# Where the halves of split weights are kept, and block inverses made for two token blocks at once: a hybrid decoder layer on one core

## The chip, the core and the metric

The kernel runs on one core of a Trainium2 chip. The core has five engines, each with its own in-order queue: TensorE (PE) multiplies matrices, VectorE (DVE) and ScalarE (ACT) work on elements, GpSimd (POOL) does so too, and SyncE (SP) issues the DMAs. The metric is the time of one execution on the device in microseconds (us); lower is better. The time before is a median of three runs.

## The reference

One decoder layer over 2048 tokens of width 1024. A projection of the input feeds three mixers: a gated DeltaNet of four heads (GDN), a dilated window attention and a differential attention. Their outputs go through `w_out` into a layer norm; a feed-forward stage with a short convolution and a second norm follow. The part that the change touches is the GDN, in chunks of tokens:

```python
a_mat = jnp.eye(C) + m                        # m: strictly lower, k k^T times decay
u = triangular_solve(a_mat, v * beta)         # the kernel makes the inverse of a_mat
w = triangular_solve(a_mat, k_beta * exp(g))
def step(S, inp):                             # over the chunks, in order
    v_new = u_i - w_i @ S
    o = q_i @ S + qk_i @ v_new
    S = S * exp(g_last) + k_tail.T @ v_new
```

The reference uses chunks of 64; the kernel uses chunks of 128, which computes the same.

## The kernel before

The 2048 tokens are four blocks of 512. Products are made in two parts: `Dense.weights` (L119 to L138) loads a raw weight tile of 128 x 1024 (512 KB), ScalarE casts it to a head `whi` (L132), GpSimd subtracts to get the rest `wlo` (L133), and a product (L174) sums three matmuls per 128 rows. Raw tile, head and rest come from one ring of seven buffers (`NW`). Where a weight has a key and `keep` is set, head and rest are also stored to DRAM (L137), and the next use of that key loads these two tiles (L127) and splits nothing. `keep` is set when the job A1 is reached (L1292).

The program is a list of jobs, `FIRST`, `SECOND` and `THIRD` (L1341 to L1343). An is the projection for the two attentions of block n (eight products and two rounds over four value weights), Gn the input of the GDN of block n (sixteen products with convolution, and gates), dn and wn the two attentions, o0 the product with `w_out` for block 0, c0 the opening of the feed-forward stage, t0 a transposition, fn the feed-forward stage of block n. A0 and G0 run before `keep` is set. `SECOND` also holds the jobs of the recurrence. in is the inverse: for each of the four chunks of block n it multiplies keys (L426), masks with the decay (L405 to L411), and stores the 32 x 32 diagonal blocks (L430); 64 of these (4 positions, 4 chunks, 4 heads) lie on 64 partitions (L435), and a loop of 31 steps with two DVE instructions each (L441, L443) inverts them; a transposed copy (L444) goes to the other 64 partitions, and both are stored (L446). bn merges the inverse of half a block (L488 and L489 load it, L498 to L518 multiply), pn prepares half a block (k and v transposed, q k), rn runs the two chunks of half a block one after the other: L530, L533, L537, L539, L542 and L545 make the state, L555 to L576 the output (L573 makes it, L576 stores it).

The order in the program is a priority. The framework lays down each engine's queue by it: work of a later job is put ahead where an earlier one isn't ready by its own estimate, and buffers come free as tiles are released. Small steps of a projection's end (norms, gates) are put off by some products with `Dense.put` and brought out by `Dense.flush`; the job in calls it with no number, which brings out everything. All DMAs are issued by SP in order. The PSUM banks of the recurrence (five) come free after r7, and the jobs of `THIRD` need them.

Of the kernel before, what the change touches and what calls it, by code (L numbers as in the profile page):

```python
# [7 lines left out]
F32 = mybir.dt.float32  # L8
F32R = mybir.dt.float32r
AF = mybir.ActivationFunctionType  # L10
ALU = mybir.AluOpType
# [365 lines left out]
def gdn_phase(tc, I, y_d, dn, cols, order, emit):  # L377
# [3 lines left out]
    with ExitStack() as ctx:  # L381
# [32 lines left out]
        def invert(t):  # L414

            qk_d = cols.blocks[t][0]
            ms = []
            blk_d = tc.dram_tile([4, 4 * H, 32, 32], F32, name="blk_d")
            for c in range(4):
                k = p2.tile([P, H, C], F32, tag="v", name="k", bufs=NV)  # L420
                nc.sync.dma_start(out=k, in_=qk_d[:, :, 0, c * C : (c + 1) * C])
                m = p2.tile([P, H, P], F32, tag="m0", name="m0", bufs=NM)
                decay(m, t, 0, c)
                kk = bank("kk")
                for h in range(H):
                    nc.tensor.matmul(out=kk[:, h], lhsT=k[:, h], rhs=k[:, h], start=True, stop=True)  # L426
                nc.vector.tensor_tensor(out=m, in0=kk, in1=m, op=ALU.mult)
                for b in range(4):
                    bs = slice(32 * b, 32 * b + 32)
                    nc.sync.dma_start(out=blk_d[b, c * H : (c + 1) * H].rearrange("q j i -> j q i"), in_=m[bs, :, bs])  # L430
                ms.append(m)
            xb = p2.tile([P, 32, 32], F32, tag="fx", name="fx", bufs=1)
            fs = p2.tile([P, 32, 32], F32, tag="fs", name="fs", bufs=1)
            mb, tmp = fs[0:64], fs[64:P]
            nc.sync.dma_start(out=mb, in_=blk_d.rearrange("b q j i -> (b q) j i"))  # L435
            nc.gpsimd.memset(xb[0:64], 0.0)
            nc.gpsimd.memset(xb[0:64].rearrange("p i c -> p (i c)")[:, 0:1024:33], 1.0)
            for j in range(31):
                n = 31 - j
                rows, cls = slice(j + 1, 32), slice(0, j + 1)  # L440
                nc.vector.tensor_tensor(out=tmp[:, rows, cls], in0=mb[:, j, rows].unsqueeze(2).broadcast_to([64, n, j + 1]),  # L441
                                        in1=xb[0:64, j, cls].unsqueeze(1).broadcast_to([64, n, j + 1]), op=ALU.mult)
                nc.vector.tensor_tensor(out=xb[0:64, rows, cls], in0=xb[0:64, rows, cls], in1=tmp[:, rows, cls], op=ALU.subtract)  # L443
            nc.vector.tensor_copy(xb[64:P], xb[0:64].rearrange("p i c -> p c i"))  # L444
            x_d = tc.dram_tile([2, 4, 4 * H, 32, 32], F32, name="x_d")
            nc.sync.dma_start(out=x_d, in_=xb)  # L446
            return ms, x_d
# [33 lines left out]
        def merge(turn, ms, x_d):  # L481

            xt = xts[turn % NXT]
            at = 2 * (turn % 2)
# [37 lines left out]
        def recur(t, hb, xt, qk, kn, vb, mq):  # L522
# [4 lines left out]
            for ci in range(2):  # L527
# [29 lines left out]
                junk = p2.tile([P, P], F32, tag="junk", name="junk", bufs=1)  # L557
# [21 lines left out]
        for job in order:  # L579
# [4 lines left out]
            elif job[0] == "b":  # L584
                merged[n] = merge(n, *inverse[n // 2])
            elif job[0] == "p":
                ready[n] = prepare(n // 2, n % 2)
            elif job[0] == "r":
                recur(n // 2, n % 2, merged.pop(n), *ready.pop(n))
            else:  # L590
                emit(job)
# [653 lines left out]
def decoder(tc, I, out, y_d=None, upto=3):  # L1245
    nc = tc.nc
    with ExitStack() as ctx:
# [11 lines left out]
        def emit(job):  # L1259
# [4 lines left out]
            elif job[0] == "G":  # L1264
                run(gi.project(n))
# [4 lines left out]
            elif job[0] == "c":  # L1270
                dn.flush()
                early.close()
# [13 lines left out]
        with ExitStack() as first:  # L1286
# [4 lines left out]
            for job in FIRST[1:]:  # L1291
                dn.keep = dn.keep or job == "A1"  # L1292
# [49 lines left out]
SECOND = "i0 b0 p0 b1 p1 r0 i1 p2 r1 p3 b2 r2 G2 i2 b3 b4 b5 r3 p4 G3 c0 r4 i3 p5 r5 p6 p7 b6 b7 r6 r7 A3 o0".split()  # L1342
# [79 lines left out]
```

## Time and profile before

| what | value |
|---|---|
| median of three runs | 3292.46 us (3285.46 to 3297.71) |
| profiled execution | 3287.69 us, of it span 3285.8 us |
| PE busy | 3039.0 us, 92% of the span |
| DVE, ACT, POOL busy | 1940.7, 1251.7, 493.0 us |
| bytes moved by DMA | 701.06 MB, mean 213 GB/s |

The page of the profile gives busy time per engine; matmuls overlap in it, so a matmul's own duration is longer than its share of the time. The granted clock is the share of full speed that TensorE was given. A stage is a stretch of the span; the table by stretch gives for each the busy time of the engines (in brackets the number of instructions), the granted clock, the share of time that the DMA engines were busy, and the rate. A wait names who waited and for what it waited last.

### The profile page before, as it was taken

Reading aid. Unit: us, or ns where it says so; the run is one execution under the profiler, and the core shown is the slowest. Engines: PE = TensorE matmul, PEld = TensorE weight load, DVE = VectorE, ACT = ScalarE, POOL = GpSimd, SP = SyncE. Lnnn points to the kernel's source line nnn. Section 1 sums busy time; section 2 is a strip of 40 time slices with the busy share of each in tenths; the row PEclk is TensorE's granted clock in tenths of the full one; section 3 lists DMA queues with packets and bytes.
Section 4 is the critical chain, followed back from the end, with each engine's and each line's share of the span. In section 5 each row is a group of like instructions: output and inputs, shape, how many; then the busy total and the mean of one; then the engine's idle time right before and its main releaser. Section 6 shows DMA issues by size and latency. Waiting matters only on the chain.

```text
span 3285.8 us, 41437 instructions
## 1 busy us (share of the span) xinstructions
PE 3039.0 (92%) x14476; PEld 2335.1 (71%) x14476; DVE 1940.7 (59%) x3738; ACT 1251.7 (38%) x2735; POOL 493.0 (15%) x342
## 2 busy tenths in 40 slices
PE   7888687999978888998999999999999999999998
PEld 5666576787767667666776667777788666788887
DVE  2564177858544536755887645565897444474446
ACT  2644143353324315644655422232655333221113
POOL 3452252111102003333312000000000000000001
PEclk8899898999988989999999999999999999999999
DMA  6437776766778878766785655555775444665553
GB/s 190 144 132 263 262 257 218 222 208 200 242 253 276 289 246 265 245 225 209 269 281 198 232 187 177 180 184 173 238 261 201 148 162 144 209 236 192 192 188 139
DMA packets 365281, 701.06 MB, mean 213 GB/s; under 512 B 63024, under 2 KB 189488, under 8 KB 364304
## 3 DMA queue, kind: packets, MB, share of 16 engines
q1 hardware_dynamic: 365072, 698.41, 64.0%
q8 instruction: 115, 1.88, 0.2%
q14 instruction: 94, 0.77, 0.1%
HBM read 525.99 MB, written 172.16 MB: 212 GB/s over the span
## 4 chain that ended last, share of the span: by engine, by line
PE 57%; DMA 7%; DVE 4%; ACT 2%; issue 2%; SPq 1%; POOL 0%; ACTq 0%; POOLq 0%; DVEq 0%
PE d L184 9%; PE d L183 9%; PE d L182 9%; PE rp L1131 6%; PE rp L1132 6%; PE rp L1134 5%; PE bank L791 4%; PE bank L806 2%; DMA wraw<-in_w_up 2%; DMA wlo<-wlo_d 2%; PE bank L970 1%; PE bank L740 1%; PE bank L977 1%; PE bank L931 1%; DMA wraw<-in_w_down 1%
## 5 line engine op out<-in xcount | busy, mean ns | idle before, releaser
L182 PE MATMUL d<-xhi,whi 128*128 128x512 f32 x2144 | 872.4, 408 | 54.7 <-DVE i_halo L336 18.1
L184 PE MATMUL d<-xhi,wlo 128*128 128x512 f32 x2144 | 866.4, 404 | 22.4 <-DMA wlo<-wlo_d 18.2
L183 PE MATMUL d<-xlo,whi 128*128 128x512 f32 x2144 | 864.9, 403 | 1.8 <-DVE xlo L145 1.7
L182 PEld LDWEIGHTS d<-xhi,whi 128*128 128x128 f32 x2144 | 416.9, 195 | 164.0 <-issue 20.3
L133 POOL TENSOR_TENSOR wlo<-wraw,whi 128x1024 fp32r<-128x1024 f32 x137 | 337.1, 2461 | 1207.7 <-ACT whi L132 1067.8
L184 PEld LDWEIGHTS d<-xhi,wlo 128*128 128x128 f32 x2144 | 415.9, 194 | 131.8 <-DMA wlo<-wlo_d 20.4
L183 PEld LDWEIGHTS d<-xlo,whi 128*128 128x128 f32 x2144 | 416.6, 194 | 105.8 <-issue 18.2
L1131 PE MATMUL rp<-whi,hhi 128*128 128x512 f32 x704 | 278.6, 400 | 6.0 <-DVE r L1141 2.3
L1132 PE MATMUL rp<-wlo,hhi 128*128 128x512 f32 x704 | 279.3, 397 | 0.0
L1134 PE MATMUL rp<-whi,hlo 128*128 128x512 f32 x672 | 263.0, 397 | 0.0
L132 ACT CAST whi<-wraw 128x1024 fp32r<-128x1024 f32 x137 | 143.6, 1048 | 281.0 <-DMA wraw<-in_w_gdn 65.2
L749 ACT ACTIVATE bank<-bank,nm 128x512 f32<-128x512 f32 (+3 forms) x320 | 190.3, 595 | 110.8 <-DVE nm L745 72.7
L745 DVE TENSOR_REDUCE nm<-bank 128x1 f32<-128x512 f32 (+3 forms) x288 | 165.4, 596 | 72.6 <-PE bank L740 70.4
L1063 ACT COPY ub<-d 128x512 f32<-128x512 f32 x172 | 100.7, 586 | 265.4 <-PE d L184 264.7
L812 DVE SCALAR_TENSOR_TENSOR pd<-pe,f_nlam,pd 128x512 f32<-128x512 f32 (+3 forms) x160 | 123.5, 786 | 124.4 <-ACT pe L808 81.5
L816 POOL TENSOR_SCALAR_AFFINE_SELECT pd<-pd 128x128 f32<-128x128 f32 x64 | 29.8, 472 | 1018.0 <-DVE pd L812 990.6
L1131 PEld LDWEIGHTS rp<-whi,hhi 128*128 128x128 f32 x704 | 133.2, 189 | 43.4 <-issue 6.3
L1132 PEld LDWEIGHTS rp<-wlo,hhi 128*128 128x128 f32 x704 | 133.3, 189 | 35.0 <-issue 8.5
L1141 DVE TENSOR_TENSOR r<-r,rp 128x512 f32<-128x512 f32 x152 | 102.3, 684 | 84.1 <-PE rp L1134 77.4
L1134 PEld LDWEIGHTS rp<-whi,hlo 128*128 128x128 f32 x672 | 127.0, 189 | 33.0 <-issue 6.5
L1064 DVE COPY c_halo<-d 128x2 f32<-128x2 f32 x172 | 26.8, 156 | 205.2 <-ACT ub L1063 205.0
L1068 DVE SCALAR_TENSOR_TENSOR yg<-ub,c_taps,yg 128x512 f32<-128x512 f32 x176 | 144.8, 823 | 3.6
(280 smaller groups left out, 4723.2 us busy)
## 6 DMA issues: line engine op xcount, KB each, us to landing
whi<-whi_d SPq DMA_DIRECT2D x291, 512.0 KB
wlo<-wlo_d SPq DMA_DIRECT2D x291, 512.0 KB
whi_d<-whi SPq DMA_DIRECT2D x101, 512.0 KB
wlo_d<-wlo SPq DMA_DIRECT2D x101, 512.0 KB
ks<-fk_d SPq DMA_DIRECT2D x160, 196.0 KB
wraw<-in_w_up SPq DMA_DIRECT2D x43, 512.0 KB
wraw<-in_w_gdn SPq DMA_DIRECT2D x32, 512.0 KB
wraw<-in_w_down SPq DMA_DIRECT2D x25, 512.0 KB
```

What stands on the lines that cost most here:

```text
L132: nc.scalar.copy(hi, raw)
L133: nc.gpsimd.tensor_tensor(out=lo, in0=raw, in1=hi, op=ALU.subtract)
L182: nc.tensor.matmul(out=ps, lhsT=whi[:, k], rhs=xhi[k], start=(k == 0), stop=False)
L183: nc.tensor.matmul(out=ps, lhsT=whi[:, k], rhs=xlo[k], start=False, stop=False)
L184: nc.tensor.matmul(out=ps, lhsT=wlo[:, k], rhs=xhi[k], start=False, stop=(k == KD - 1))
L745: nc.vector.tensor_reduce(out=o, in_=s[:, 0:nf], axis=mybir.AxisListType.X, op=ALU.min)
L749: nc.scalar.activation(out=s[:, 0:n], in_=s[:, 0:n], func=AF.Exp, scale=-1.0, bias=o, accum_out=den[:, b, m, qt : qt + 1])
L791: nc.tensor.matmul(out=po[64 * hh : 64 * hh + 64, q0:], lhsT=v[:, 64 * hh : 64 * hh + 64], rhs=pd[hh][:, q0:], start=start, stop=stop)
L1068: nc.vector.scalar_tensor_tensor(out=yc, in0=ub[:, j : j + TB], scalar=self.taps[:, mt, j : j + 1], in1=yc, op0=ALU.mult, op1=ALU.add)
L1131: nc.tensor.matmul(out=ps, lhsT=hi[:, sl], rhs=whi, start=first, stop=False)
L1132: nc.tensor.matmul(out=ps, lhsT=hi[:, sl], rhs=wlo, start=False, stop=last and lo is None)
L1134: nc.tensor.matmul(out=ps, lhsT=lo[:, sl], rhs=whi, start=False, stop=last)
```

## The change

Three things. `keep` is set in the job c0, so heads and rests are stored from there on only: those of A1 and G1 are not stored, G1, G2 and G3 load and split raw tiles, and A3 stores its weights for A2. The inverse is made for two blocks at once: i0 for blocks 0 and 1, i1 for blocks 2 and 3, with the 128 small blocks on 128 partitions; the product of a step lies in rows of the input already used, or for the first five steps in a tile `ft` of 136 columns, which the recurrence's `junk` shares. The order of `SECOND` is another, and each job Gn begins with a flush.

```diff
-        def invert(t):
-            qk_d = cols.blocks[t][0]
+        def invert(pair):
             ms = []
-            blk_d = tc.dram_tile([4, 4 * H, 32, 32], F32, name="blk_d")
-            for c in range(4):
+            blk_d = tc.dram_tile([4, 8 * H, 32, 32], F32, name="blk_d")
+            for n in range(8):
+                t, c = 2 * pair + n // 4, n % 4
                 k = p2.tile([P, H, C], F32, tag="v", name="k", bufs=NV)
-                nc.sync.dma_start(out=k, in_=qk_d[:, :, 0, c * C : (c + 1) * C])
+                nc.sync.dma_start(out=k, in_=cols.blocks[t][0][:, :, 0, c * C : (c + 1) * C])
...
-                    nc.sync.dma_start(out=blk_d[b, c * H : (c + 1) * H].rearrange("q j i -> j q i"), in_=m[bs, :, bs])
+                    nc.sync.dma_start(out=blk_d[b, n * H : (n + 1) * H].rearrange("q j i -> j q i"), in_=m[bs, :, bs])
                 ms.append(m)
             xb = p2.tile([P, 32, 32], F32, tag="fx", name="fx", bufs=1)
-            fs = p2.tile([P, 32, 32], F32, tag="fs", name="fs", bufs=1)
-            mb, tmp = fs[0:64], fs[64:P]
+            mb = p2.tile([P, 32, 32], F32, tag="fs", name="fs", bufs=1)
             nc.sync.dma_start(out=mb, in_=blk_d.rearrange("b q j i -> (b q) j i"))
-            nc.gpsimd.memset(xb[0:64], 0.0)
-            nc.gpsimd.memset(xb[0:64].rearrange("p i c -> p (i c)")[:, 0:1024:33], 1.0)
+            nc.gpsimd.memset(xb, 0.0)
+            nc.gpsimd.memset(xb.rearrange("p i c -> p (i c)")[:, 0:1024:33], 1.0)
             for j in range(31):
                 n = 31 - j
                 rows, cls = slice(j + 1, 32), slice(0, j + 1)
-                nc.vector.tensor_tensor(out=tmp[:, rows, cls], in0=mb[:, j, rows].unsqueeze(2).broadcast_to([64, n, j + 1]),
-                                        in1=xb[0:64, j, cls].unsqueeze(1).broadcast_to([64, n, j + 1]), op=ALU.mult)
-                nc.vector.tensor_tensor(out=xb[0:64, rows, cls], in0=xb[0:64, rows, cls], in1=tmp[:, rows, cls], op=ALU.subtract)
-            nc.vector.tensor_copy(xb[64:P], xb[0:64].rearrange("p i c -> p c i"))
-            x_d = tc.dram_tile([2, 4, 4 * H, 32, 32], F32, name="x_d")
-            nc.sync.dma_start(out=x_d, in_=xb)
+                used = mb.rearrange("p j i -> p (j i)") if j > 4 else p2.tile([P, 136], F32, tag="ft", name="ft", bufs=1)
+                tmp = used[:, 0 : n * (j + 1)].rearrange("p (a b) -> p a b", a=n)
+                nc.vector.tensor_tensor(out=tmp, in0=mb[:, j, rows].unsqueeze(2).broadcast_to([P, n, j + 1]),
+                                        in1=xb[:, j, cls].unsqueeze(1).broadcast_to([P, n, j + 1]), op=ALU.mult)
+                nc.vector.tensor_tensor(out=xb[:, rows, cls], in0=xb[:, rows, cls], in1=tmp, op=ALU.subtract)
+            nc.vector.tensor_copy(mb, xb.rearrange("p i c -> p c i"))
+            x_d = tc.dram_tile([2, 4, 8 * H, 32, 32], F32, name="x_d")
+            nc.sync.dma_start(out=x_d[0], in_=xb)
+            nc.sync.dma_start(out=x_d[1], in_=mb)
             return ms, x_d
...
-            at = 2 * (turn % 2)
+            at = 2 * (turn % 4)
...
-                junk = p2.tile([P, P], F32, tag="junk", name="junk", bufs=1)
+                junk = p2.tile([P, 136], F32, tag="ft", name="junk", bufs=1)[:, 0:P]
...
-                merged[n] = merge(n, *inverse[n // 2])
+                merged[n] = merge(n, *inverse[n // 4])
...
             elif job[0] == "G":
+                dn.flush()
                 run(gi.project(n))
...
             elif job[0] == "c":
                 dn.flush()
+                dn.keep = True
                 early.close()
...
             for job in FIRST[1:]:
-                dn.keep = dn.keep or job == "A1"
                 emit(job)
...
-SECOND = "i0 b0 p0 b1 p1 r0 i1 p2 r1 p3 b2 r2 G2 i2 b3 b4 b5 r3 p4 G3 c0 r4 i3 p5 r5 p6 p7 b6 b7 r6 r7 A3 o0".split()
+SECOND = "i0 b0 p0 b1 p1 r0 b2 p2 r1 G2 b3 p3 r2 G3 c0 i1 r3 p4 p5 b4 b5 r4 b6 r5 A3 p6 p7 b7 r6 r7 o0".split()
```

## Rows read from the trace of the kernel before

**Rows 1.** Stages: us busy of PE, PEld, DVE, ACT, POOL; clock, DMA share, GB/s

```profile
118.00:240.00 122.00, 110.50 (x462) 84.44 (x462) 82.25 (x99) 59.65 (x108) 68.45 (x50) 0.94 0.38 117
240.00:395.00 155.00, 122.25 (x580) 91.51 (x581) 52.70 (x113) 45.02 (x84) 33.55 (x18) 0.87 0.80 264
395.00:545.00 150.00, 125.30 (x543) 101.49 (x541) 111.16 (x175) 58.48 (x124) 67.06 (x43) 0.88 0.75 252
545.00:870.00 325.00, 302.23 (x2102) 252.50 (x2103) 229.60 (x495) 129.19 (x329) 52.43 (x60) 0.95 0.68 213
870.00:1000.00 130.00, 107.13 (x665) 90.72 (x663) 56.94 (x135) 38.87 (x114) 11.52 (x13) 0.88 0.78 251
1000.00:1095.00 95.00, 78.09 (x446) 61.32 (x446) 45.31 (x92) 34.02 (x86) 21.13 (x11) 0.89 0.87 297
```

**Rows 2.** Waits of PE in A1: us, times, longest

```profile
PE vp L628 <- ACT whi L132: 10.8, 2, 6.5
PE d L182 <- ACT whi L132: 5.9, 1, 5.9
```

**Rows 3.** Waits of SP's queue in A1

```profile
SPq L137 <- ACT whi L132: 22.5, 8, 10.5
SPq L137 <- POOL wlo L133: 7.6, 6, 2.1
```

**Rows 4.** Waits of SP's queue in G1

```profile
SPq L137 <- ACT whi L132: 34.2, 12, 7.4
```

**Rows 5.** Waits of PE in G1

```profile
PE d L182 <- DVE i_halo L336: 12.3, 2, 6.2
```

**Rows 6.** DVE in G1: what, count | busy us, mean ns | idle

```profile
L341 DVE SCALAR_TENSOR_TENSOR yc<-ub,i_taps,yc 128x512 f32<-128x512 f32 x36 | 38.7, 1075 | 1.0
L441 DVE TENSOR_TENSOR fs<-fs,fx 64x31 f32<-64x31 f32 (+15 forms) x31 | 18.0, 579 | 1.0
L443 DVE TENSOR_TENSOR fx<-fx,fs 64x31 f32<-64x31 f32 (+15 forms) x31 | 15.7, 506 | 1.0
```

**Rows 7.** DVE in G2 and G3

```profile
L341 DVE SCALAR_TENSOR_TENSOR yc<-ub,i_taps,yc 128x512 f32<-128x512 f32 x72 | 57.5, 798 | 1.8
L441 DVE TENSOR_TENSOR fs<-fs,fx 64x31 f32<-64x31 f32 (+15 forms) x62 | 24.1, 388 | 6.9 <-DMA fs<-blk_d 5.0
L443 DVE TENSOR_TENSOR fx<-fx,fs 64x31 f32<-64x31 f32 (+15 forms) x62 | 23.4, 378 | 2.0
```

**Rows 8.** Groups by line over the whole span

```profile
L133 POOL TENSOR_TENSOR wlo<-wraw,whi 128x1024 fp32r<-128x1024 f32 x137 | 337.1, 2461 | 1207.7 <-ACT whi L132 1067.8 <-ACT ub L1062 53.1 <-DMA wlo_d<-wlo 33.1
...
L132 ACT CAST whi<-wraw 128x1024 fp32r<-128x1024 f32 x137 | 143.6, 1048 | 281.0 <-DMA wraw<-in_w_gdn 65.2 <-DMA wraw<-in_w_att 57.4 <-DMA wraw<-in_w_val 46.3
...
L427 DVE TENSOR_TENSOR m<-kk,m 128x512 f32<-128x512 f32 x16 | 11.0, 687 | 11.2 <-POOL m L411 10.4 <-PE kk L426 0.7
...
L363 DVE TENSOR_TENSOR nsb<-nsb,nps 8x512 f32<-8x512 f32 x12 | 8.0, 669 | 2.7 <-PE nps L359 2.7
```

**Rows 9.** Chain that ended last, one piece: start us, us, what

```profile
986.75 1.09 PE pk L530 x8
```

**Rows 10.** Stores of gates and inverses: ns (min/median/max), first to last start

```profile
L299 SPq DMA_DIRECT2D at_d<-at x4: 329/336/394, 432.1 to 864.5; - x4
...
L446 SPq DMA_DIRECT2D x_d<-fx x4: 320/323/2690, 536.8 to 947.1; - x4
```

**Rows 11.** Timeline of DVE, outputs of r0, r5, r6, r7: start us, us

```profile
622.43 0.74 DVE L573 SCALAR_TENSOR_TENSOR yo<-yp,g_nwh,z 128x512 f32<-128x512 f32 x1
...
982.06 0.75 DVE L573 SCALAR_TENSOR_TENSOR yo<-yp,g_nwh,z 128x512 f32<-128x512 f32 x1 [0.86 <-PE yp L571]
...
1029.71 0.74 DVE L573 SCALAR_TENSOR_TENSOR yo<-yp,g_nwh,z 128x512 f32<-128x512 f32 x1
...
1063.85 0.75 DVE L573 SCALAR_TENSOR_TENSOR yo<-yp,g_nwh,z 128x512 f32<-128x512 f32 x1 [0.33 <-PE yp L571]
...
1074.23 0.75 DVE L573 SCALAR_TENSOR_TENSOR yo<-yp,g_nwh,z 128x512 f32<-128x512 f32 x1 [1.70 <-DMA z<-z_d]
```

## The prediction

> **What bounds the kernel now.** I read the page first, then a table of busy time by stage, then who waited for whom in each stage, then single lines. The page gives TensorE (PE) 92% of the span, so a gain can only be PE time that is idle or slow. The table by stage [rows 1] shows where that is; I cut the stages from the order of the weight loads: the first gated projection G0 with the attention of block 0 (118 to 240), projections A1 (240 to 395), G1 (395 to 545), G2 and G3 (545 to 870), A3 (870 to 1000), the output product o0 (to 1095). I call PE busy time times granted clock the stage's work, and work over length its rate. G0: 110.50 x 0.94 = 103.9 of 122, rate 0.852. A1: 122.25 x 0.87 = 106.4 of 155, 0.686. G1: 110.3 of 150, 0.735. G2 and G3: 287.1 of 325, 0.883. A3 and o0: 94.3 + 69.5 = 163.8 of 225, 0.728. The granted clock (the mean of stretches at 2.4 and at 1.2 GHz) falls to 0.87 and 0.88 where PE was idle most, so a stall is paid twice. From 1095 on the diff leaves the work as it is.
>
> Why A1 is slow: PE's own waits there are for casts of weights [rows 2], and the DMA queue of SyncE (SP), which issues everything in order, stands before the stores of L137 until the cast and the subtraction are made: 22.5 + 7.6 us in A1 [rows 3], 34.2 us in G1 [rows 4]. Whatever is queued behind (the next raw weight, the stores of the conv outputs) stands too. In G1 PE's largest wait is for the halo copy of VectorE (DVE) [rows 5]: there the inverse of block 0 runs between the convolutions, 18.0 + 15.7 us of DVE [rows 6].
>
> **The change part by part.** (a) Stores. `keep` is set at c0 instead of A1, so A1's 12 weights and G1's 16 are no longer written (56 stores of 512 KB); A3's 12 are written instead (24 stores). G1, G2 and G3 load one raw tile, 512 KB, and split it; before, G2 and G3 loaded two halves, 1 MB. Traffic: 16 weights x 1 MB of stores less, 48 loads of 0.5 MB instead of 1 MB less, 40 MB of 701. For A1 I take G0's rate, the stage of [rows 1] with raw loads and no store: 106.4 / 0.852 = 125 us, a gain of 30. Bounds: 8 (half of the 16.7 us of [rows 2] goes) and 35 (rate 0.883). G1 also loses the inverse loop, since i0 now needs block 1's gates: 110.3 / 0.852 = 129.5, a gain of 20; bounds 6 (half of [rows 5]) and 25.
>
> (b) New splits. 48 weights (4 in A1, 16 each in G2 and G3, and 12 in A3) are cast and subtracted again: 48 x 1.05 = 50 us of ScalarE and 48 x 2.46 = 118 us of GpSimd [rows 8]. Both have room (129 and 52 of 325 us in G2 and G3 [rows 1]). What it costs is on DVE, which runs longer instructions while GpSimd works: the convolution L341 takes 1075 ns in G1 [rows 6] and 798 in G2 and G3 [rows 7]; L441 takes 579 against 388, L443 506 against 378. Summed over G1: 36 x 0.277 + 31 x 0.191 + 31 x 0.128 = 19.9 us for 16 subtractions, 1.24 us each. So 32 of them put 40 us on DVE in G2 and G3. A raw weight also holds three of the seven weight buffers rather than two; G0 ran so, and its rate has that in it.
>
> The Trainium skill (SBUF — State Buffer, "Who interferes with whom") says that a DVE instruction with two SBUF inputs contends with a GpSimd instruction that reads SBUF, and that the one that came second is blocked until the other ends. The trace agrees in kind: L341, L441 and L443 have two inputs in SBUF. By the rule alone a subtraction can hold DVE for its whole 2.46 us, 79 us for 32 of them instead of 40; the measured 1.24 decides.
>
> (c) Inverses by pairs. One loop of 62 instructions on 128 partitions replaces two on 64. That the partitions cost nothing is read from L363 on 8 partitions, 669 ns, and L427 on 128, 687 ns, with the same 512 elements [rows 8]. In G2 and G3 one loop goes, (24.1 + 23.4) / 2 = 23.8 us of DVE [rows 7]. DVE there: 229.6 + 40 - 23.8 = 246 of 325 us, 0.76; G1 had 0.74 [rows 1] and rate 0.735, with stores, and G0 0.67 and 0.852. I take 0.80 for G2 and G3, between G1 and 0.883; ends 0.735 and 0.883.
>
> (d) Order. Inverse i1 (blocks 2 and 3) starts only when G3 is made, and merges b4 to b7 and recurrences r4 to r7 follow it; before, i2 (r4, r5) was made before G3. So r3, b4, b5 and p4 move behind G3. A recurrence has twelve groups like the one of [rows 9], 1.09 us each, 13 us; a merge and a preparation I estimate at 5 us each, as four or five such groups: 28 us of PE. G2 and G3: (287.1 - 28) / 0.80 = 324 us, a gain of 1. The gates of block 3, 864.5 [rows 10], come at 864.5 - 30 - 20 - 1 = 813.
>
> From there a chain runs, by rows: gates to the inverse's store 947.1 - 864.5 = 82.6 [rows 10]; that store to the next recurrence's first output, 1029.7 - 947.1 = 82.6 (536.8 to 622.4 for r0, 85.6); from recurrence to recurrence 34.1 and 47.7; from the last one's first output to its second 10.4 [rows 11]. Before, two recurrences hang behind the last inverse, now four. 813 + 82.6 + 82.6 + 3 x 34.1 + 10.4 = 1091; with 40.9, the mean, 1111. The short end is PE's work: (163.8 + 28) / 0.852 = 225, so 1038. Before, the stage ended at 1095. I take 1080, nearer to the chain because its rows are direct, below it because the rows were taken with the kept loads of A3 and two other recurrences in the queues; block 2's half of i1 can be made ahead. That is 15 us sooner than 1095; ends 57 sooner and 16 later.
>
> What A3's stores add is a wait: SP stands before each for 1.25 us on average (30.1 us over 24 in [rows 3]), and behind it stand the merges' loads (L488, L489) and z for the recurrences. 30 us of SP in A3; A3 can be made while i1 runs, so I cost it at nothing; if that cover is gone, up to 30 us in the chain.
>
> (e) Flush before each G, and `ft` for `junk`: the gates' chain of the block before is brought out earlier, among matmuls that don't need it: nothing; uncovered one stall like those of [rows 5], 6 us.
>
> **Sum.** -30 - 20 - 1 up to block 3's gates, +36 behind them: -15. The profiled run took 3287.7 us (span 3285.8 and 1.9 around it), which gives 3272.7; it lies 4.8 below the median 3292.5, and counted from there it is 3277.5. I name 3275.
>
> **The rivals.** *The tail decides* (slower): r4 to r7 follow at 47.7 us, as r6 did after r5: 813 + 165.2 + 143 + 10.4 = 1132, +37, 3325 to 3330; A3's stores can add more. For it: SP is in order and A3's stores lie there; against it: there is less in the queues. It decides from a pace of 35 us on, where the chain reaches 1095. *DVE becomes the bound in G2 and G3*: they run at G1's 0.735, 259.1 / 0.735 = 352, 28 us more than in the sum: +13, 3301 to 3305. For it: DVE at 0.76. This is also where the skill's rule on the two engines would lead, with 79 us in place of 40. *All relief reaches the end*: A1, G1, G2 and G3 at 0.883 give 539 of 630 us, a gain of 91, and the rest 225 as before: 3197. For it: 40 MB and 34 + 30 us of SP waits go. Against it: no stage with raw loads has run so. *It changes nothing*: raw loads wait for buffers where stores stood, and PE with them: 3288 to 3292.
>
> **How the numbers follow.** Forecast 0.38, tail 0.22, all relief 0.20, DVE 0.17, nothing 0.03. A measurement tells about 0.5%, 16 us, from no change: faster is below 3276, slower above 3309. The forecast lies at that bound, so 0.20 of it is faster and 0.18 the same. Faster 0.20 + 0.20 = 0.40; same 0.18 + 0.13 + 0.03 = 0.34; slower 0.22 + 0.04 = 0.26. The range: 3222 leaves out the lower half of the full relief, 3325 the upper part of the tail.
>
> **What would show it.** In A1 and G1: L137 gone from SP's waits, PE's waits for whi under half, clock above 0.92. In G2 and G3: L341 above 1000 ns, PE waits for the halo copy. Behind G3: one inverse's store about 165 us before the first of four outputs that follow at 34 to 41 us. I am wrong if A1 and G1 stay at 305 us, or if the last output of the recurrences lies after 1095.

## The result, and the profile after

The changed kernel takes 3307.36 us (median of seven runs, 3300.94 to 3309.66) beside 3285.46 for the kernel before on the same chip: ratio 1.0064, 95% interval 1.0043 to 1.0085. It is slower by 0.64%, where 3275 and rather faster was forecast. The profiled run took 3306.08 us, its span is 3304.2; before, 3285.8.

The stages of the changed kernel, cut at its own gates and inverses: 237 to 372 is A1, 372 to 503 G1, 503 to 825 G2 and G3, 825 to 911 from block 3's gates to the store of the second inverse, 981 to 1100 the last recurrences and o0. Columns as in [rows 1].

```profile
237.00:372.00 135.00, 118.16 (x582) 89.60 (x583) 55.31 (x114) 52.28 (x93) 48.14 (x23) 0.95 0.59 185
372.00:503.00 131.00, 107.31 (x479) 87.66 (x479) 89.61 (x113) 59.65 (x117) 68.53 (x43) 0.94 0.54 170
503.00:825.00 322.00, 288.48 (x1772) 237.00 (x1771) 227.82 (x386) 140.43 (x320) 131.47 (x86) 0.93 0.48 148
825.00:911.00 86.00, 61.30 (x311) 50.19 (x309) 45.50 (x105) 24.44 (x69) 13.21 (x11) 0.82 0.71 217
911.00:981.00 70.00, 49.17 (x497) 40.98 (x498) 16.88 (x37) 18.25 (x42) 12.45 (x6) 0.78 0.68 210
981.00:1100.00 119.00, 101.91 (x670) 84.02 (x669) 63.18 (x125) 51.96 (x136) 31.75 (x20) 0.96 0.88 302
```

A1 and G1 run at a clock of 0.95 and 0.94 (0.87 and 0.88 in [rows 1]) with the DMA engines at 0.59 and 0.54 instead of 0.80 and 0.75. The place that gets worse is 825 to 981: clock 0.82 and 0.78. The waits of SP's queue in A1 and G1, the longest three, then PE's largest wait in A1:

```profile
SPq L345 <- DVE th L344: 33.1, 10, 6.8
SPq L130 <- PE d L183: 20.7, 6, 5.3
SPq L130 <- PE d L184: 17.0, 4, 10.2
```

```profile
PE vp L631 <- ACT whi L132: 7.5, 3, 3.3
```

The stores of L137 [rows 3, 4] are gone from the queue. SP now stands before raw loads (L130) until a buffer is free, and before the stores of the conv outputs (L345) for DVE.

DVE in G2 and G3 (as [rows 7]), then GpSimd's subtractions, then PE's waits there:

```profile
L341 DVE SCALAR_TENSOR_TENSOR yc<-ub,i_taps,yc 128x512 f32<-128x512 f32 x72 | 74.0, 1028 | 1.4
L338 DVE TENSOR_SCALAR yc<-ub,i_taps 128x512 f32<-128x512 f32 x24 | 29.8, 1240 | 0.0
...
L443 DVE TENSOR_TENSOR fs<-fs,fx 128x156 f32<-128x156 f32 (+15 forms) x26 | 17.9, 687 | 0.4
```

```profile
L133 POOL TENSOR_TENSOR wlo<-wraw,whi 128x1024 fp32r<-128x1024 f32 x32 | 78.0, 2436 | 96.5 <-ACT whi L132 92.3 <-PE d L184 4.2
```

```profile
PE d L182 <- DVE i_halo L336: 8.2, 2, 7.9
PE yp L574 <- POOL on L571: 5.3, 4, 3.4
PE ntp L368 <- DVE nsb L363: 3.3, 1, 3.3
...
PE vp L473 <- DVE mq L479: 2.9, 3, 1.7
PE pv L540 <- DVE R L536: 2.6, 2, 1.5
PE kp L471 <- DVE vb L478: 2.5, 2, 2.3
```

The convolution L341 takes 1028 ns (798 in [rows 7]), and PE's waits there now mostly name DVE: summed over all of PE's waits above 60 ns between the gates of block 1 and block 3, 21.4 us are for DVE, against 5.6 before. Those before:

```profile
PE kp L468 <- DVE vb L475: 2.7, 1, 2.7
...
PE d L182 <- DVE i_halo L336: 2.3, 1, 2.3
...
PE po L552 <- DVE S L545: 0.6, 1, 0.6
```

The timeline of both engines shows how it comes about (start, duration):

```profile
612.31 2.34 POOL L133 TENSOR_TENSOR wlo<-wraw,whi 128x1024 fp32r<-128x1024 f32 x1 [1.67 <-ACT whi L132]
612.58 0.68 DVE L363 TENSOR_TENSOR nsb<-nsb,nps 8x512 f32<-8x512 f32 x1 [3.16 <-PE nps L359]
...
626.76 2.38 POOL L133 TENSOR_TENSOR wlo<-wraw,whi 128x1024 fp32r<-128x1024 f32 x1 [7.49 <-ACT whi L132]
627.19 2.50 DVE L344 SCALAR_TENSOR_TENSOR th<-th,yc 128x512 f32<-128x512 f32 x1 [0.77 <-ACT th L343]
...
635.78 2.36 POOL L133 TENSOR_TENSOR wlo<-wraw,whi 128x1024 fp32r<-128x1024 f32 x1 [3.38 <-ACT whi L132]
...
636.30 2.12 DVE L338 TENSOR_SCALAR yc<-ub,i_taps 128x512 f32<-128x512 f32 x1
```

Where nothing is beside it, L344 takes 0.69 us. Begun at 627.19, behind the subtraction of 626.76 to 629.14, it ends at 629.69, 0.55 us after GpSimd is through. L338, 0.47 us where nothing is beside it, ends 0.28 us after the subtraction. L363, whose second input lies in PSUM, runs its 0.68 us through a subtraction untouched. So in these rows DVE stands nearly the whole time that a subtraction has left. Counted through that trace, 27 of the 32 subtractions between the gates of block 1 and block 3 catch a DVE instruction like this, which then takes about 1.6 us more than it takes alone, 44 us in all; 11 of the instructions caught are L338, 7 are L341. The other five subtractions meet only instructions with an input in PSUM, or none.

Gates are stored at 370.2, 502.8, 673.3 and 824.8 us [rows 10: 432.1 to 864.5], the inverses at 588.9 and 910.4.

### The profile page after: what moved, and what is told of

Same layout as the page of the kernel before. It is cut to its first block, busy times and chain, and to the rows that moved or that the text cites. A ratio compares the mean times of both kernels' runs of the same rounds, so it can differ in the third digit from the quotient of the medians.

```text
span 3304.2 us, 41273 instructions
## 1 busy us (share of the span) xinstructions
PE 3036.8 (92%) x14476; PEld 2330.7 (71%) x14476; DVE 1943.7 (59%) x3612; ACT 1296.2 (39%) x2781; POOL 607.8 (18%) x386
## 5 line engine op out<-in xcount | busy, mean ns | idle before, releaser
L133 POOL TENSOR_TENSOR wlo<-wraw,whi 128x1024 fp32r<-128x1024 f32 x185 | 451.8, 2442 | 1362.4 <-ACT whi L132 1188.2
L132 ACT CAST whi<-wraw 128x1024 fp32r<-128x1024 f32 x185 | 193.8, 1048 | 375.1 <-DMA wraw<-in_w_gdn 94.1
L341 DVE SCALAR_TENSOR_TENSOR yc<-ub,i_taps,yc 128x512 f32<-128x512 f32 x144 | 152.6, 1060 | 3.4
L794 PE MATMUL bank<-pd,fv 128*64 128x512 f32 (+3 forms) x320 | 141.7, 554 | 0.8 <-POOL pd L819 0.6
```

Source lines behind the costliest of these rows:

```text
L132: nc.scalar.copy(hi, raw)
L133: nc.gpsimd.tensor_tensor(out=lo, in0=raw, in1=hi, op=ALU.subtract)
L341: nc.vector.scalar_tensor_tensor(out=yc, in0=ub[:, j : j + TB], scalar=self.taps[:, mt, j : j + 1], in1=yc, op0=ALU.mult, op1=ALU.add)
L794: nc.tensor.matmul(out=po[64 * hh : 64 * hh + 64, q0:], lhsT=v[:, 64 * hh : 64 * hh + 64], rhs=pd[hh][:, q0:], start=start, stop=stop)
```

## The experiments

One measure is used throughout. PE does the same matmuls in every kernel (14476 records in each trace); with each matmul counted at its duration at full clock, I read from the matmul records when each kernel has done as much work as the kernel before has at a given time. The difference is its lead (minus) or lag. It is read from one execution of each kernel and swings by some 10 us between neighbouring marks (the changed kernel leads by 37 us at 520, 44 at 530 and 33 at 540), so a difference of that size is a hint and no more. Between the gates of block 1 and of block 3, a stretch that holds G2, G3 and whatever else was laid there, I also give the length: 312.8 us before, 322.0 after. A caution for all: the framework lays the queues anew for each edit, so more than the edited instruction moves.

| kernel | median us | ratio to before, 95% interval | gates 1 to 3, us |
|---|---|---|---|
| changed kernel | 3307.36 | 1.0064 (1.0043 to 1.0085) | 322.0 |
| x1 stores alone | 3303.52 | 1.0049 (1.0029 to 1.0068) | 357.9 |
| x2 pairs and order alone | 3274.44 | 0.9961 (0.9946 to 0.9975) | 287.0 |
| x3 no stores in A3 | 3308.92 | 1.0058 (1.0036 to 1.0080) | 323.3 |
| x4 first pair only | 3274.29 | 0.9961 (0.9945 to 0.9976) | 352.6 |
| x5 G1's weights kept | 3258.37 | 0.9911 (0.9891 to 0.9932) | 289.5 |
| x6 x4 and G1's weights kept | 3250.65 | 0.9895 (0.9879 to 0.9911) | 313.9 |
| x7 rests filled | 3248.07 | 0.9892 (0.9867 to 0.9916) | 285.9 |
| x8 second loop left out | 3297.62 | 1.0034 (1.0019 to 1.0049) | 324.8 |
| x9 rests filled three times | 3262.71 | 0.9929 (0.9912 to 0.9946) | 289.2 |
| x10 32 rests on DVE | 3246.62 | 0.9879 (0.9864 to 0.9894) | 289.0 |
| x11 x1 and G1's weights kept | 3268.23 | 0.9943 (0.9927 to 0.9959) | 321.8 |
| x12 all rests on DVE | 3241.75 | 0.9858 (0.9823 to 0.9892) | 289.5 |
| x13 x4, 32 rests on DVE | 3256.75 | 0.9928 (0.9904 to 0.9951) | 317.2 |
| x14 x10, no stores in A3 | 3262.97 | 0.9943 (0.9924 to 0.9963) | 287.1 |

### The two halves of the change

**x1** takes from the change only the place where `keep` is set; inverses, order and flush are those of before.

```diff
             elif job[0] == "c":
                 dn.flush()
+                dn.keep = True
...
-                dn.keep = dn.keep or job == "A1"
```

> The first half of the change alone: head and rest are kept from c0 on, inverses stay single, the order of the jobs is that of before. Theory 1 (the pair is what costs: four recurrences instead of two hang behind the gates of block 3): the gain in A1 and G1 stays (the gates of block 3 near 825 to 835 us instead of 864), the last output of the recurrences comes about 210 us later as before, and the time is 3245 to 3265. Theory 2 (the stores and raw tiles of A3, which now stand in the stage of the recurrences, are what costs): A3 stalls here as well, and the time is 3280 to 3305. Theory 3 (the 32 new splits in G2 and G3 hold up VectorE): from the gates of block 1 to those of block 3 it takes over 330 us, and the time is 3280 to 3305 too.

**x2** is the changed kernel with `keep` set at A1, as before.

```diff
-                dn.keep = True
...
+                dn.keep = dn.keep or job == "A1"
```

> The second half alone: inverses by pairs and the new order, but head and rest kept from A1 on, as before. Theory 1: the tail behind the gates of block 3 is as long as in the changed kernel (about 275 us from gates to the last output), A1 stays slow, G1 gains some 15 us because no inverse runs in it; 3305 to 3330. Theory 2: A3 loads kept halves and stores nothing, so the tail shrinks to about 245 us; 3280 to 3300.

x1 is 0.5% slower, x2 0.4% faster. In x1 PE leads by 21 us at 395 (the end of A1 in [rows 1]), by 30 at 450, by 20 at 550, and lags by 13.5 at 850: 33 us are lost in G2 and G3, and gates 1 to 3 take 357.9 us. So leaving out the stores brings most of what was forecast for A1, and leaving the rests to be made again costs more than that. x2 shows no such loss: gates 1 to 3 in 287.0 us. It also brings block 1's gates 24 us sooner (528.0), with all stores in place, though its PE work is then only 8 ahead: the gates come sooner by the order and the flush rather than by work done; which of the two brings them, no run separates.

### The stores of A3, and the order

**x3** sets `keep` in o0 instead of c0: A3 stores nothing and splits its four value weights once for each round, and A2 splits raw weights. Since `keep` is set by then, A2 also stores its halves, which nothing loads later: its trace has 170 stores of L137, as many as the changed kernel's. So the 24 stores of A3 are moved to A2 and not taken away.

```diff
             elif job[0] == "c":
                 dn.flush()
-                dn.keep = True
...
             elif job[0] == "o":
+                dn.keep = True
```

> The changed kernel with keep set at o0 instead of c0: A3 stores nothing (24 stores of 512 KB fewer in the stage of the recurrences), and A2 loads and splits raw tiles. Theory 1: the chain of four recurrences sets the tail; gates to last output stays within 10 us of 275, and the time is 3297 to 3310. Theory 2: PE's waits for whi and wlo in A3 (22 us in the changed kernel) and the queue of SyncE before the stores fall away; 3275 to 3292.

**x4** makes the pair for blocks 0 and 1 only; blocks 2 and 3 get single inverses (`invert_one`, the inverse of the kernel before), nearly in the order before.

```diff
-                inverse[n] = invert(n)
+                inverse[n] = invert(0) if n == 0 else invert_one(n) + (2,)
...
-SECOND = "i0 b0 p0 b1 p1 r0 b2 p2 r1 G2 b3 p3 r2 G3 c0 i1 r3 p4 p5 b4 b5 r4 b6 r5 A3 p6 p7 b7 r6 r7 o0".split()
+SECOND = "i0 b0 p0 b1 p1 r0 b2 p2 r1 G2 i2 b3 p3 r2 b4 b5 r3 p4 G3 c0 r4 i3 p5 r5 p6 p7 b6 b7 r6 r7 A3 o0".split()
```

> The changed kernel with the pair for blocks 0 and 1 only; blocks 2 and 3 have single inverses in the order of before from G2 on, so r4 and r5 no longer wait for the gates of block 3. Theory 1: gates to last output falls from 275 to 205 to 220 us, and the time is 3250 to 3270. Theory 2: no more than 10 us of the 22 come back; 3295 to 3310.

x3: between 850 and 950 PE loses 39 us against the kernel before, where the changed kernel loses 53; so A3's stores cost some 14 us at their place, not much more than the swing of that measure. At the end nothing is left of it. x4 gains 33 us over the changed kernel, which then looked as if the second pair were at fault; x13 below takes that back.

### The splits of G2 and G3

**x5** is the changed kernel in which G1 stores its sixteen weights again and G2 and G3 load them; A1's stay out of DRAM. **x6** does so in x4.

```diff
...
-        if key is not None and self.keep:
+        if key is not None and (self.keep or key[0] == "gdn" and self.keep_gdn):
...
             elif job[0] == "G":
+                dn.keep_gdn = n > 0
```

> The changed kernel, but G1 stores heads and rests of its 16 weights again, and G2 and G3 load them (A1 still stores nothing, A3 still stores). If the raw tiles and splits of G2 and G3 are what costs there (x1_stores_only needed 358 us from the gates of block 1 to those of block 3 where the kernel before needed 313): those gates come 285 to 295 us apart instead of 322, G1 loses 5 to 12 us, and the time falls to 3275 to 3292. If they are not (the order of the jobs or the pair is): no change, 3300 to 3312.

> x4_pair_first (a pair for blocks 0 and 1, single inverses for blocks 2 and 3) with G1's weights kept as in x5_gdn_kept. If the costs are separate (raw tiles in G2 and G3 about 20 to 30 us, the second pair about 30), this one has neither: 3245 to 3262. If one cost only hides the other: 3270 to 3280, as x4_pair_first and x2_pairs_only gave.

**x7** keeps loads, casts and buffers of the changed kernel and lets GpSimd fill the rests of G2 and G3 with zeros in place of the subtraction; the rest's part of those products is left out of what is computed.

```diff
-        nc.gpsimd.tensor_tensor(out=lo, in0=raw, in1=hi, op=ALU.subtract)
+        nc.gpsimd.memset(cast(lo), 0.0) if self.no_rest else nc.gpsimd.tensor_tensor(out=lo, in0=raw, in1=hi, op=ALU.subtract)
...
-                dn.flush()
-                run(gi.project(n))
+                dn.flush(); dn.no_rest = n > 1
+                run(gi.project(n)); dn.no_rest = False
```

> The changed kernel in which GpSimd fills the rests of G2's and G3's 32 weights with zeros instead of subtracting (those rests are left out of the sum), so that raw tiles, casts, buffers and DMAs stay and only GpSimd's 2.4 us of reading two tiles goes. If VectorE standing still behind GpSimd is what raw tiles cost in G2 and G3: the mean of L341 between the gates of block 1 and those of block 3 falls from over 1000 ns to under 850, the gates come 295 to 305 us apart instead of 322, and the time is 3280 to 3295. If it is the raw tiles' way (three buffers a weight, cast after load): 3300 to 3312.

x5 is 49 us faster than the changed kernel and x7 59 us. x7 has the same traffic, loads and casts, so it is the 32 subtractions that cost this, neither bytes nor buffers; that it is not the zeros in x7's products, x10 shows, which computes everything. Gates 1 to 3, first the changed kernel, then x5 and x7:

```profile
502.80:824.80 322.00, 288.48 (x1772) 236.99 (x1771) 227.81 (x386) 140.63 (x320) 131.47 (x86) 0.93 0.48 148
```

```profile
504.50:794.00 289.50, 277.38 (x1788) 231.45 (x1787) 189.77 (x395) 119.25 (x296) 62.60 (x57) 0.97 0.67 219
```

```profile
496.70:782.60 285.90, 275.05 (x1762) 230.97 (x1761) 185.77 (x382) 143.94 (x321) 86.58 (x86) 0.96 0.52 164
```

With about the same work, DVE is busy 227.8 us with the subtractions and 185.8 without: 42 us for 32 of them, 1.3 each.

**x8** leaves the loop of the second pair out (31 steps, 62 DVE instructions), so the inverses of blocks 2 and 3 aren't computed; all else of the chain stands.

```diff
-            for j in range(31):
+            for j in range(0 if pair else 31):
```

> The changed kernel without the 31 steps of the second pair's loop (the inverses of blocks 2 and 3 are left out); loads, stores, merges and recurrences stay. If the chain from the gates of block 3 through the second pair sets the tail: that pair's stores come 25 to 45 us sooner, the last output as much, and the time is 3268 to 3285. If TensorE has other work enough (A3, o0) and is held by its weights instead: the stores come sooner too, but the time stays at 3297 to 3310.

The later store of the second inverse (L449) comes at 866.6 instead of 911.5 and the last output of the recurrences 22 us sooner, at 1076.2 instead of 1098.1. At the end the median is 10 us lower, with intervals that overlap. So the chain behind block 3's gates is at most a part of what sets the time.

### Which of GpSimd's properties costs

**x9** is x7 with three fills for each rest, so GpSimd is as busy as with a subtraction and the rest as late, but nothing is read from SBUF. What x7 leaves out is left out here too.

```diff
-        nc.gpsimd.tensor_tensor(out=lo, in0=raw, in1=hi, op=ALU.subtract)
+        [nc.gpsimd.memset(cast(lo), 0.0) for _ in range(3)] if self.no_rest else nc.gpsimd.tensor_tensor(out=lo, in0=raw, in1=hi, op=ALU.subtract)
```

> As x7, the rests of G2 and G3 are filled with zeros by GpSimd instead of subtracted, but with three fills one after the other, 3 x 0.95 = 2.9 us a weight, longer than the subtraction's 2.44; the rest's part of those products is left out of the computation. GpSimd is as busy as in the changed kernel and the rest comes as late, but GpSimd reads nothing from SBUF. If the cost of the subtractions is that VectorE is held while GpSimd reads: L341 between 780 and 850 ns and 3245 to 3262 us, ratio 0.988 to 0.994. If it is GpSimd's time and the late rest: 3290 to 3310 us, ratio 1.001 to 1.007.

**x10** computes everything, with the 32 subtractions of G2 and G3 on VectorE.

```diff
-        nc.gpsimd.tensor_tensor(out=lo, in0=raw, in1=hi, op=ALU.subtract)
+        (nc.vector if self.dve_rest else nc.gpsimd).tensor_tensor(out=lo, in0=raw, in1=hi, op=ALU.subtract)
...
-                dn.flush()
-                run(gi.project(n))
+                dn.flush(); dn.dve_rest = n > 1
+                run(gi.project(n)); dn.dve_rest = False
```

> The changed kernel with the 32 subtractions of G2 and G3 on VectorE instead of GpSimd. On VectorE one takes about 2 x 0.68 = 1.37 us (from 0.68 us for 512 columns, L145), 32 of them 44 us; in exchange the 1.24 us by which each held VectorE from GpSimd's side, 40 us, go. If VectorE's time is what the stretch is bound by: about as the changed kernel, 3295 to 3315 us, ratio 1.003 to 1.009. If what cost was that the rest is ready late (2.4 us on GpSimd against 1.4): 3255 to 3285 us, ratio 0.99 to 1.0.

x9, gates 1 to 3: the stretch, GpSimd's fills, DVE's L341, and PE's two largest waits.

```profile
505.40:794.60 289.20, 274.68 (x1765) 230.51 (x1764) 195.60 (x385) 143.38 (x321) 142.86 (x144) 0.96 0.51 161
```

```profile
L133 POOL MEMSET wlo<- 128x1024 f32 x87 | 84.4, 972 | 45.9 <-PE d L184 43.4
```

```profile
L341 DVE SCALAR_TENSOR_TENSOR yc<-ub,i_taps,yc 128x512 f32<-128x512 f32 x72 | 60.7, 843 | 1.3
L338 DVE TENSOR_SCALAR yc<-ub,i_taps 128x512 f32<-128x512 f32 x24 | 25.8, 1074 | 0.0
```

```profile
PE yp L574 <- POOL on L571: 10.0, 4, 7.4
PE po L555 <- DVE S L548: 1.4, 1, 1.4
```

GpSimd is busier than in the changed kernel (142.9 against 131.5 us), and still 45 of the 59 us are gained; PE waits 2.0 us for DVE instead of 21.4. What is left, 3262.7 - 3248.1 = 15 us, is the smaller part. It holds the time that GpSimd itself needs (PE's wait of 10.0 us above names it) and L338, which the fills still lengthen. x10, the same views:

```profile
501.20:790.20 289.00, 274.69 (x1765) 229.40 (x1765) 220.42 (x411) 143.57 (x323) 72.08 (x57) 0.97 0.51 160
```

```profile
L341 DVE SCALAR_TENSOR_TENSOR yc<-ub,i_taps,yc 128x512 f32<-128x512 f32 x72 | 60.6, 841 | 1.1
L133 DVE TENSOR_TENSOR wlo<-wraw,whi 128x1024 fp32r<-128x1024 f32 x29 | 37.8, 1305 | 14.3 <-ACT whi L132 14.0
```

```profile
PE ntp L368 <- DVE nsb L363: 5.5, 2, 3.0
PE t1p L501 <- DMA g_xlow<-x_d: 3.2, 1, 3.2
```

DVE makes the subtraction in 1305 ns, GpSimd in 2436; and DVE's busy time hardly differs (220.4 us here, 227.8 after; 1937.0 and 1943.7 over the whole span). Held by GpSimd, DVE pays as much as for doing the work. Yet x10 is 61 us faster than the changed kernel and beats both kernels. I had expected a time like that of the changed kernel if DVE's time were the bound: it isn't; nor did I expect less than 3255. PE waits 8.7 us for DVE, between the 2.0 of x9 and the 21.4 of the changed kernel. DVE's share is 0.71 in the slow kernel and 0.76 in the fast one.

**x12** moves all 185 subtractions to VectorE.

```diff
-        nc.gpsimd.tensor_tensor(out=lo, in0=raw, in1=hi, op=ALU.subtract)
+        nc.vector.tensor_tensor(out=lo, in0=raw, in1=hi, op=ALU.subtract)
```

> The changed kernel with all 185 subtractions of rests on VectorE, not only the 32 of G2 and G3 as in x10 (3246.6 us). 67 of the others lie before 503 us, 18 in A3, o0 and behind them, 68 in the feed-forward stage. If a subtraction on GpSimd costs the kernel wherever TensorE stands at times, as it did in G2 and G3 (61 us for 32, 1.9 each): 30 to 130 us more are gained from the 85 outside the feed-forward stage, 3115 to 3215 us, ratio 0.947 to 0.978. If it costs only where the inverse's loop and the recurrences run short VectorE steps beside it, in G2 and G3: 3235 to 3255 us, ratio 0.984 to 0.991. If VectorE then is too full (68 x 1.3 = 88 us more in the feed-forward stage): above 3255 us.

3241.75 us, the lowest of all; its interval overlaps that of x10. 153 more subtractions moved, and no gain that can be told at the end. By PE's work x12 is 8 us ahead of x10 at 450, 4 ahead at 1250 and 4 behind at 2000. So a price that lasts is seen for G2 and G3 alone, where the inverse's loop, the recurrences and the convolutions share DVE; that this sharing is the reason is argued, not tried.

### What belongs to the pairs

**x11** is x1 with G1's weights kept (the edit of x5), the fourth corner to x1, x4 and x6.

```diff
...
-        if key is not None and self.keep:
+        if key is not None and (self.keep or key[0] == "gdn" and self.keep_gdn):
...
             elif job[0] == "G":
+                dn.keep_gdn = n > 0
```

> x1 (order and inverses as before, no pairs) with the weights of G1 stored and loaded in G2 and G3, as x5 does for the changed kernel. It is the fourth corner: x1 3303.5 and x4 3274.3 have the splits in G2 and G3, x6 3250.7 has not. If a pair's gain is the VectorE time that it saves, it is worth less where VectorE has room: 3250 to 3262 us here, ratio 0.989 to 0.993, and the splits cost 42 to 53 us without pairs. If it is the order of the jobs: 29 us above x6 here too, 3273 to 3286 us, ratio 0.996 to 1.0.

Its 3268.2 lies between the two ranges: with the weights of G1 kept the first pair and its order are worth 18 us (x6), without 29 (x1 against x4).

**x13** is x4 and **x14** is x3, each with the edit of x10:

```diff
-        nc.gpsimd.tensor_tensor(out=lo, in0=raw, in1=hi, op=ALU.subtract)
+        (nc.vector if self.dve_rest else nc.gpsimd).tensor_tensor(out=lo, in0=raw, in1=hi, op=ALU.subtract)
...
-                dn.flush()
-                run(gi.project(n))
+                dn.flush(); dn.dve_rest = n > 1
+                run(gi.project(n)); dn.dve_rest = False
```

> x4 (a pair for blocks 0 and 1, single inverses for 2 and 3) with the subtractions of G2 and G3 on VectorE, as in x10 (3246.6 us, both pairs). With the subtractions on GpSimd, x4 lay 33 us below the changed kernel; with the weights of G1 kept, x6 lay 8 below x5. If the second pair costs in the tail, whatever runs in G2 and G3: 33 us below x10, 3205 to 3225 us, ratio 0.975 to 0.982. If its cost was that its order suffers from the subtractions on GpSimd: 3235 to 3250 us, ratio 0.984 to 0.990.

> x10 (subtractions of G2 and G3 on VectorE) with the storing of heads and rests set from o0 on, so that A3 stores nothing and A2 splits raw weights, as x3 does for the changed kernel. A3's stores took about 14 us at their place (820 to 960 us) there, with nothing left of it at the end. If they reach the end here: 3228 to 3238 us, ratio 0.982 to 0.985. If A2 pays it back: 3240 to 3258 us, ratio 0.986 to 0.991.

Gates 1 to 3 of x4 and, with the subtractions on DVE, of x13:

```profile
502.50:855.10 352.60, 314.17 (x2118) 259.02 (x2117) 266.13 (x482) 149.20 (x350) 130.08 (x89) 0.92 0.48 145
```

```profile
502.10:819.30 317.20, 297.83 (x2043) 247.33 (x2042) 255.30 (x498) 147.36 (x334) 75.11 (x59) 0.95 0.52 159
```

In that stretch the price of the subtractions is about the same in three orders: 322.0 - 289.0 = 33 us with two pairs, 352.6 - 317.2 = 35 with one (some 6 of it because x4 has 75 matmuls more in its stretch than x13), 357.9 - 321.8 = 36 with none (x11, by keeping). At the end it is 61, 18 and 35 us by the medians, and 61, 11 and 35 by the ratios, each taken beside the kernel before on its own chip. With G2 and G3 undisturbed the second pair shows no cost: x13, without it, is slower than x10, the opposite of x4 against the changed kernel, while x6, without it too, is 8 us below x5 with intervals that overlap. x14 is slower than x10 by 16 us. By PE's work it leads by 36 us at 1100 and by 16 at 1150, where x10 has 28 at both: A2, which splits and stores its weights there, pays more than A3 saved. How much of that is A2's splits and how much its useless stores, no run separates.

x2, x5, x7 and x10 came out below both of the ranges written down for them, x13 and x14 above both, x4 and x11 between.

## Why the prediction was wrong, step by step

By PE's work, the changed kernel leads by 35 us at 550 (A1 and G1 done), by 19 at 850 (G2 and G3 done), lags by 33 at 950 and by 12 to 24 from 1250 on; the end is 18.4 later. The forecast said -50, -51 and, at the end, -15. Step by step that is -35 instead of -50 for A1 and G1, +16 instead of -1 for G2 and G3, and +37 behind them, where the sum had +36. So the steps that failed are G1 in (a), put too high by 10 us and more, and above all G2 and G3 in (c), put at -1 where 16 us were lost; the last number fits by luck, as (d) shows.

**(a) Stores: A1 nearly right, G1 too high.** A1 was put at -30; the lead is 26 at 395, the end of A1 in [rows 1], and 21 in x1 (32 and 30 at 450, inside G1). G1 was put at -20 and gave 10. Its rate is 107.31 x 0.94 / 131 = 0.77, where G0's 0.852 was forecast. The stages as cut by each kernel's own marks give 39 us together (155 and 150, then 135 and 131). Block 1's gates did come 49 us sooner, as 50 was forecast, but x2 shows that 24 of them come with the new order alone: I counted the loop that leaves G1 as gained, when its work and that of the jobs around it only went elsewhere. The signs for this step came true: L137 is gone from SP's waits, PE's waits for whi in A1 fell from 16.7 to 7.5 us, the clock came to 0.95 and 0.94, and A1 and G1 take 266 us.

**(b) The subtraction's hold on DVE: the size was right, in part by luck.** 1.24 us were forecast, 1.3 measured. The forecast added up L341, L441 and L443 alone; of the 42 us by which DVE's busy time falls in x7, about 11 are L338 and 4 are L344, which it left out. The Trainium skill (SBUF — State Buffer, "Who interferes with whom") says that the instruction that came second is blocked until the other ends, and that a GpSimd instruction that only writes doesn't hold a DVE instruction with two inputs. The trace agrees with both: the rows at 627.19, and L341 at 843 ns beside the fills of x9 against 1028. That it is 1.3 us on average and not the subtraction's 2.4 the count above explains: five of 32 catch nothing, and the others catch an instruction that begins some time after the subtraction. L338, caught most often, has one input tensor and not two.

**(c) G2 and G3: length right, gain wrong; this step failed.** I forecast 324 us for them and set this against 325, cut at 545 and 870. Gates 1 to 3, the stretch meant, took 312.8 before and 322.0 after: +9, not -1, with r3, b4, b5 and p4 moved out of it. By PE's work 16 us are lost there. At its place even the price in the sum was right: from rate 0.883 to 0.80 it was 259.1 / 0.80 - 259.1 / 0.883 = 30 us; x10 shows 33. What I missed is that the stretch without the subtractions was worth more: with the subtractions off GpSimd the rate is 274.69 x 0.97 / 289 = 0.92, not 0.883, and that at the end 61 us are lost for 33 at the place. The rival "DVE becomes the bound", 3301 to 3305, comes nearest to 3306 in number, but its own mechanism, G1's rate of 0.735, didn't occur: 288.48 x 0.93 / 322 = 0.83.

**(d) The tail: the chain was right, and I set it against another mark.** By rows it was 82.6 + 82.6 + 3 x 34.1 + 10.4 = 278 us from block 3's gates. Measured: the inverse's store after 85.6 us, and then DVE's outputs (timeline of DVE, as [rows 11]), the first of r4, r5, r6 and r7 and the last of all:

```profile
983.37 0.75 DVE L576 SCALAR_TENSOR_TENSOR yo<-yp,g_nwh,z 128x512 f32<-128x512 f32 x1 [2.34 <-PE yp L574]
...
1024.10 0.74 DVE L576 SCALAR_TENSOR_TENSOR yo<-yp,g_nwh,z 128x512 f32<-128x512 f32 x1
...
1058.58 0.75 DVE L576 SCALAR_TENSOR_TENSOR yo<-yp,g_nwh,z 128x512 f32<-128x512 f32 x1 [0.93 <-PE yp L574]
...
1090.11 0.75 DVE L576 SCALAR_TENSOR_TENSOR yo<-yp,g_nwh,z 128x512 f32<-128x512 f32 x1 [0.47 <-PE yp L574]
1098.07 0.75 DVE L576 SCALAR_TENSOR_TENSOR yo<-yp,g_nwh,z 128x512 f32<-128x512 f32 x1
```

85.6, 73.0, a pace of 40.7, 34.5 and 31.5, and 8.0 for the last output: 273.3 us. (The sign "one inverse's store about 165 us before the first of four outputs" is a slip: 165 runs from the gates, the store lies 82.6 before; measured 158.6 and 73.0.) Here the sum was put together wrongly: the chain's end, 1091 by its rows, was first pulled down to 1080, then compared with 1095, the end of a stage that holds o0 too. The same mark before is the last output, 1074.2 [rows 11]. Mark against mark the chain gave +17 even with the gates at 813; they came at 824.8, and the last output 23.8 us later than before. My sentence "wrong if the last output lies after 1095" came true. But nor is this mark the cause of the time: x2 has its last output at 1113.1, later than the changed kernel, and is 33 us faster; x8 cuts the chain by 22 and gains 10, with intervals that overlap. So it is luck that +36 comes near the 37 us lost behind 850, and luck too that +17 would have named the time. The rival "tail decides" priced a pace of 47.7 us; it was 36 on average, just above the 35 from which it said that it decides, but x2 and x8 speak against its mechanism.

**(d), A3's stores, costed at nothing, and (e):** some 14 us at their place in x3; moved to A2, where nothing loads what they wrote, they leave the end as it was (x3) or 16 us later (x14). The flush was not tried by itself; x2 suggests that it brings the gates sooner.

**The cause.** The change gains some 30 us in A1 and G1 by not storing, and gives up twice that by having GpSimd subtract while DVE is needed for the convolutions, the loop and the recurrences of G2 and G3 (x7, x9, x10, and x5 from the other side). With these 32 subtractions on DVE the same change is 1.2% faster than the kernel before. What stays open is why 33 to 36 us lost in the stretch become 11 to 61 at the end, by the order of the jobs. By PE's work, of what x10 gains on the changed kernel some 34 us are there at 850, 40 at 1100, 51 at 1250 and 60 at 2000, though behind 850 both run the same instructions; that the hold causes this part too is not shown, and the queues laid anew by each edit make it hard to separate.

## What to carry to other kernels

Busy share doesn't price an engine: look at who waits for it, and at single instructions that take three times their usual time beside another engine's. A two-input elementwise step that GpSimd makes while DVE works on PE's short chains can cost more than the same step made on DVE itself, even when DVE looks fuller. When a forecast ends in a chain, set its last event against the same event of the kernel before, and count a job that moves out of a stage as moved, not gained.

## What the runs showed of the hardware that was not expected

A subtraction of 128 x 1024 on GpSimd (2436 ns) takes DVE about as much time as making it there (1305 ns): DVE's busy time over the span is 1943.7 us with 32 on GpSimd and 1937.0 with them on DVE. Fills, which only write, leave the two-input L341 alone (843 ns) but not L338, a tensor_scalar: 1074 ns beside the fills of x9, 1240 beside subtractions. It goes the other way too: GpSimd's own cast of 128 x 512 (0.61 us where nothing holds it) can be held by DVE. First the changed kernel, then x10:

```profile
L350 POOL CAST isqh<-isq 128x512 fp32r<-128x512 f32 x16 | 12.1, 758 | 37.9 <-ACT isq L348 37.9
```

```profile
L350 POOL CAST isqh<-isq 128x512 fp32r<-128x512 f32 x16 | 24.6, 1538 | 85.5 <-ACT isq L348 85.5
```

Two casts of x10 make most of that difference, 3.5 and 8.5 us long (x7 and x9 have one of 4.1 each). The longer one stands beside DVE instructions that follow one another without a pause, a subtraction among them, and ends 0.47 us after their first pause begins (566.25 to 566.40):

```profile
558.20 8.52 POOL L350 CAST isqh<-isq 128x512 fp32r<-128x512 f32 x1 [21.92 <-ACT isq L348]
```

```profile
565.85 0.40 DVE L445 TENSOR_TENSOR fx<-fx,fs 128x247 f32<-128x247 f32 x1
566.40 1.41 DVE L133 TENSOR_TENSOR wlo<-wraw,whi 128x1024 fp32r<-128x1024 f32 x1
```

The median of the sixteen casts is 0.61 us in the changed kernel and 0.80 in x10.
